# Joining two of the three matmuls of a Strassen product, and moving two weight sums to GpSimd

## The chip, the core and the metric

The kernel runs on one core of a Trainium2 chip. The core has five engines with a queue of instructions each: TensorE (PE in the profile, its weight loads are PEld), VectorE (DVE), ScalarE (ACT), GpSimd (POOL) and SyncE (SP, which here only issues DMAs). An engine takes the instructions of its queue in order; a semaphore wait of one holds back all that stand behind it. The metric is the device time of one execution in microseconds (us), the median of several runs. Lower is better.

## The reference

A streaming encoder: two layers on 512 tokens of 1024 features, all in float32. In each layer

```
x = x + 0.5 * swiglu(rms_norm(x, g1), w_gate, w_up, w_down)      # FFN 1, inner width 2816
h = rms_norm(x, gm);  p = h @ w_in
x = x + concat(attention(p), conv(p)) @ w_out                    # the mixer
x = x + 0.5 * swiglu(rms_norm(x, g2), w_gate, w_up, w_down)      # FFN 2
x = rms_norm(x, gp)

def swiglu(x, w_gate, w_up, w_down):
    return (silu(x @ w_gate) * (x @ w_up)) @ w_down
```

There are four FFNs in all. The change lies in their gate and up products; the mixer is not touched.

## The kernel before

**Split precision.** A float32 factor is held as a high part in the type that TensorE multiplies (`hi`, a cast on ScalarE) and the remainder (`lo`, a subtraction on VectorE). A product of two such factors is three matmuls that accumulate in PSUM: hi x hi, hi x lo and lo x hi (`mm3`, L152 to L154; the first two load the same weights, `wh`, and stream the activation's hi and lo part).

**An FFN.** `ffn_body` treats the inner width in four chunks of blocks, `CHUNKS = ((0, 2), (2, 5), (5, 8), (8, 11))`; a unit of a chunk is a pair of 128-wide inner blocks, gate and up. The first chunk is computed plainly, with matmuls of 512 columns. Meanwhile `operands` builds the activations' Strassen combinations for all later pairs. The other three chunks have three pairs each; each pair goes through `pair`, so that there are 9 pairs in an FFN and 36 in the kernel. After the chunks (2, 5) and (5, 8) the down projection of that chunk follows as `down`, two rounds (g = 0, 1) of seven Strassen products too, and for these chunks `pair` also builds the down operands from its results (`quartered`: the tiles b, u, v and their splits). The last chunk is followed by a plain down projection.

**A pair.** Winograd's form of Strassen: the weights come as four quarters of 128x1024 (a11, a12, a21, a22, loaded by SP), the activations as b11, b21, t2, t3, t1, t4, b22. There are seven products, in this order, each into one of three PSUM banks:

- b11 with a11 into bx, b21 with a12 into by
- t2 with s2 into bx (added to what is there), t3 with s3 into bz, t1 with s1 into bx
- t4 with a22 into bz, b22 with s4 into bx

A product is 2 (gate and up, `gu`) x 4 (k) x 3 matmuls of 128x256: gate fills columns 0 to 255 of the bank, up the columns 256 to 511. Before bx is added to again, its partial sum is copied out by ScalarE (`copied`), and VectorE combines the copies (L389, L400, L402, L406 and so on).

**The weights' side.** `split_into` makes hi (ACT, L242) and lo (DVE, L244) of a quarter or of a sum, five times in a pair. For a12 and a22, `summed` takes lo another way: ACT writes the negated hi (L366) and GpSimd issues a DMA that adds the weights from HBM to it (L367). The four sums of quarters s3, s1, s2, s4 are made in place on VectorE (L385 to L388), each 128x1024: s3 = a11 + a21, then a21 = a21 + a22, a11 = a11 + a21, a12 = a12 + a11.

**Order.** A scheduler with a time model of its own places the instructions in the queues. `tc.issue_after` adds fixed edges on one engine: products keep their order on TensorE, and the sums stand behind the last VectorE operation on the previous pair's t1 product (`order["first"]`). Pools set the rest: 7 PSUM banks, 4 weight tiles `wh` and 4 `wl`, 4 quarter tiles `fr`, 3 `raw` (a12 and s3 lie there), 2 `ls`, 5 `tmps`.

Of the kernel before, what the change touches and what calls it, by code (L numbers as in the profile page):

```python
# [7 lines left out]
FP = mybir.dt.float32  # L8
# [7 lines left out]
P = 128  # L16
# [41 lines left out]
ORDER = "t0s1p3v4o5"  # L58

# [13 lines left out]
def encoder_kernel(ctx: ExitStack, tc: tile.TileContext, xT, consts, vecs, rgain, wgu1, wd1, wdq1,  # L73
# [11 lines left out]
    def nm(s):  # L85
        uid[0] += 1
        return f"{s}{uid[0]}"
# [163 lines left out]
    def ffn_body(fpool, l, gx, norm, wgu, wd, wdq, gain, done, w0, halved):  # L251
# [52 lines left out]
        def operands(R):  # L304

            def halved(src, own=False):
                hi, lo = (fpool.tile([P, S], FR, tag="xs", name=nm("xs"), bufs=2) if own else slot(FR)
                          for _ in range(2))
                h3, l3 = (v.rearrange("p (j t) -> p j t", j=2) for v in (hi, lo))
                A.copy(h3, src)  # L310
                V.tensor_tensor(l3, src, h3.bitcast(FP), ALU.subtract)
                return hi, lo
# [5 lines left out]
            for i in range(2):  # L318
# [7 lines left out]
                for n, src in (("b11", b11), ("b21", b21)):  # L326
                    X[n].append(halved(src))
                    yield
# [4 lines left out]
                X["t2"].append(halved(t2))  # L333
                yield
                X["t3"].append(halved(t3))
# [3 lines left out]
                X["t1"].append(halved(t1))  # L339
# [3 lines left out]
                X["t4"].append(halved(t4))  # L343
                yield
                X["b22"].append(halved(b22, i == 1))
                yield

        def product(o, w, n, start, stop):
            with tc.issue_after(order["pe"]):
                for gu in range(2):  # L350
                    for k in range(4):
                        hi, lo = X[n][k // 2]
                        t = slice(k % 2 * HS, (k % 2 + 1) * HS)
                        c = slice(gu * 512 + k * P, gu * 512 + (k + 1) * P)
                        last = mm3(o[:, gu * HS:(gu + 1) * HS], w[0][:, c], w[1][:, c], hi[:, t], lo[:, t],
                                   start and gu == 0 and k == 0, stop and k == 3, True)
            order["pe"] = last

        def copied(o, src):
            A.copy(o, src)  # L360
            return o

# [14 lines left out]
        def pair(p, quartered):  # L377

            a11, a12, a21, a22, s3 = quarters(wgu[l, p], WC, p == CHUNKS[0][1])
            bx, by, bz = bank(), bank(), bank()  # L380
# [3 lines left out]
            with after("first"):  # L384
                V.tensor_tensor(s3, a11, a21, ALU.add)  # L385
                V.tensor_tensor(a21, a21, a22, ALU.add)
                V.tensor_tensor(a11, a11, a21, ALU.add)  # L387
                V.tensor_tensor(a12, a12, a11, ALU.add)  # L388
            V.tensor_tensor(a, a, by, ALU.add)  # L389
            s = tmp()  # L390
            A.activation(s[:, 0:HS], a[:, 0:HS], AF.Silu)
# [3 lines left out]
            copied(r2[:, 0], bx)  # L395
            product(bz, split_into("s3", s3), "t3", True, True)
            d = copied(tmp(), bz)
            product(bx, split_into("s1", a21), "t1", False, True)
# [808 lines left out]
```

## Time and profile before

| what | value |
|---|---|
| median of 3 runs (lowest to highest) | 1806.97 us (1805.7 to 1807.44) |
| span of the profiled execution | 1803.8 us, 3.2 us under the median |
| TensorE busy, matmuls | 1786.7 us (99%), 12198 |
| VectorE busy | 1423.3 us (79%) |
| ScalarE busy | 1088.8 us (60%) |
| GpSimd busy | 422.2 us (23%) |
| one matmul 128x256, mean duration in the record | 282 ns |
| one matmul 128x512 (L153), mean duration in the record | 389 ns |

The span runs from the first instruction's start to the last one's end in one profiled execution; the median is of whole executions. Matmuls are pipelined, so the duration in a record is longer than the time from one matmul's start to the next one's; what a matmul costs in a full queue is read from successive starts in the timeline. A row of the timeline is: start and length in us, engine, line, operation, written tile <- read tiles, shape, and in brackets the idle time ahead of it with what ended it. A row of the windows has, for each engine, the busy time in that stretch and the number of instructions.

### The profile page before, as it was taken

The page shows a single profiled execution, that of the slowest core. Times are in us where ns is not written, and L with a number is a line of the kernel's source. Part 1 is how long each engine was busy: PE and PEld are TensorE (multiplying, and loading weights), DVE is VectorE, ACT ScalarE, POOL GpSimd, SP SyncE. Part 2 cuts the span into 40 slices and gives each one's busy share as a digit, 9 for nine tenths or more (in the row PEclk, how much of TensorE's full clock was granted, in tenths as well). Part 3 has the DMA queues.
Part 4 walks back from the last instruction along what each step waited for, and adds up shares of the span by engine and source line. Part 5 has one row for each costly group of instructions (what it writes and reads, how often), then busy time and mean ns, then how long its engine had stood idle before and what let it go on. Part 6 is the DMA issues. An engine that isn't in the chain of part 4 may idle for free.

```text
span 1803.8 us, 30598 instructions
## 1 busy us (share of the span) xinstructions
PE 1786.7 (99%) x12198; PEld 1645.8 (91%) x12198; DVE 1423.3 (79%) x1975; ACT 1088.8 (60%) x1685; POOL 422.2 (23%) x343
## 2 busy tenths in 40 slices
PE   9999999999999999999999999999999999999998
PEld 7899999888788899999888999998978788999997
DVE  7888887588956979887779888866999668888873
ACT  5565656457953565656635656554779535656564
POOL 1000000258843000000310000002589410000001
PEclk9999999999999999999999999999999999999999
DMA  5657574324102466664326575743250126575742
GB/s 172 165 132 193 123 187 112 108 88 135 31 24 99 126 163 162 151 163 126 123 65 170 122 195 121 194 110 110 80 147 6 52 79 167 129 189 126 187 112 73
DMA packets 70415, 226.23 MB, mean 125 GB/s; under 512 B 7936, under 2 KB 8320, under 8 KB 70272
## 3 DMA queue, kind: packets, MB, share of 16 engines
q1 hardware_dynamic: 54000, 169.74, 28.1%
q0 software_dynamic: 16128, 54.53, 17.7%
q8 instruction: 95, 1.56, 0.4%
q14 instruction: 48, 0.39, 0.1%
q10 hardware_dynamic: 144, 0.00, 0.0%
HBM read 222.15 MB, written 2.10 MB: 124 GB/s over the span
## 4 chain that ended last, share of the span: by engine, by line
PE 80%; DVE 8%; ACT 5%; POOL 3%; issue 3%; DMA 1%; SPq 0%; ACTq 0%; POOLq 0%; DVEq 0%
PE ps L154 26%; PE ps L152 25%; PE ps L153 25%; POOL y L896 2%; PE ps L834 1%; DVE wl L244 1%; ACT pr L892 1%; DVE x L449 1%; DVE r L160 1%; ACT r L806 1%; PE ps L800 1%; DVE wl L142 1%; DVE cv L888 1%; DMA raw<-in_wgu 1%; ACT wh L136 1%
## 5 line engine op out<-in xcount | busy, mean ns | idle before, releaser
L153 PE MATMUL ps<-r,wh 128*128 128x256 f32 (+1 forms) x3436 | 1062.3, 309 | 0.1
L152 PE MATMUL ps<-r,wh 128*128 128x256 f32 (+1 forms) x3436 | 1061.0, 311 | 0.6 <-ACT r L159 0.3
L154 PE MATMUL ps<-r,wl 128*128 128x256 f32 (+1 forms) x2668 | 845.6, 318 | 2.6 <-DVE wl L142 1.2
L152 PEld LDWEIGHTS ps<-r,wh 128*128 128x128 f32 x3436 | 650.9, 190 | 38.6 <-ACT wh L136 2.1
L153 PEld LDWEIGHTS ps<-r,wh 128*128 128x128 f32 x3436 | 652.3, 190 | 36.4 <-issue 2.4
L154 PEld LDWEIGHTS ps<-r,wl 128*128 128x128 f32 x2668 | 506.9, 190 | 41.3 <-DVE wl L142 3.0
L136 ACT CAST wh<-raw 128x1024 fp32r<-128x1024 f32 (+3 forms) x148 | 132.1, 900 | 211.0 <-issue 101.3
L367 POOL DMA_DIRECT2D ls<-in_wgu x72 | 62.5, 869 | 741.7 <-ACT ls L366 615.3
L242 ACT CAST wh<-fr 128x1024 fp32r<-128x1024 f32 (+1 forms) x160 | 157.6, 985 | 101.5 <-DVE fr L387 39.7
L142 DVE TENSOR_TENSOR wl<-raw,wh 128x1024 fp32r<-128x1024 f32 (+3 forms) x132 | 146.8, 1117 | 91.0 <-ACT wh L136 90.0
L154 PE MATMUL ps<-r,ls 128*128 128x256 f32 x768 | 216.7, 282 | 0.0
L244 DVE TENSOR_TENSOR wl<-fr,wh 128x1024 fp32r<-128x1024 f32 (+1 forms) x160 | 182.9, 1143 | 40.3 <-ACT wh L242 40.3
L896 POOL TENSOR_TENSOR y<-y,pr 128x511 f32<-128x511 f32 (+14 forms) x120 | 157.4, 1312 | 54.6 <-ACT pr L892 47.4
L154 PEld LDWEIGHTS ps<-r,ls 128*128 128x128 f32 x768 | 145.2, 189 | 0.0
L244 DVE TENSOR_TENSOR wl<-raw,wh 128x1024 fp32r<-128x1024 f32 (+1 forms) x100 | 113.7, 1137 | 24.6 <-ACT wh L242 24.1
L189 POOL TENSOR_TENSOR r<-r,t 128x512 f32<-128x512 f32 x45 | 77.4, 1728 | 172.7 <-ACT t L185 171.9
L242 ACT CAST wh<-raw 128x1024 fp32r<-128x1024 f32 (+1 forms) x100 | 97.9, 979 | 27.9 <-PE ps L153 19.9
L366 ACT ACTIVATE ls<-fr 128x1024 fp32r<-128x1024 f32 (+1 forms) x56 | 56.1, 1002 | 78.6 <-PE ps L154 65.2
L892 ACT ACTIVATE pr<-r,vec 128x511 f32<-128x511 f32 (+14 forms) x120 | 85.3, 735 | 10.1 <-POOL y L896 10.1
L888 DVE SCALAR_TENSOR_TENSOR cv<-r,vec,cv 128x511 f32<-128x511 f32 (+14 forms) x120 | 88.0, 733 | 3.4 <-ACT cv L884 2.1
L449 DVE SCALAR_TENSOR_TENSOR x<-ps,x 128x512 f32<-128x512 f32 x112 | 77.1, 689 | 15.8 <-PE ps L154 15.4
L367 POOL DMA_DIRECT2D ls<-in_wdq x32 | 27.6, 863 | 260.5 <-ACT ls L366 260.5
(220 smaller groups left out, 2441.5 us busy)
## 6 DMA issues: line engine op xcount, KB each, us to landing
fr<-in_wgu SPq DMA_DIRECT2D x112, 512.0 KB, 3.4
ls<-in_wgu POOLq DMA_DIRECT2D x72, 512.0 KB, 6.3
raw<-in_wgu SPq DMA_DIRECT2D x62, 512.0 KB, 5.0
fr<-in_wdq SPq DMA_DIRECT2D x48, 384.0 KB, 4.6
ls<-in_wdq POOLq DMA_DIRECT2D x32, 384.0 KB, 4.7
raw<-in_wd SPq DMA_DIRECT2D x32, 384.0 KB, 3.1
raw<-in_wd SPq DMA_DIRECT2D x32, 256.0 KB, 2.7
raw<-in_wcv SPq DMA_DIRECT2D x16, 512.0 KB, 3.2
```

Of the source, the lines that this page charges most:

```text
L136: order["cast"] = A.copy(hi[:, :w], raw[:, :w]).ins
L142: (G if kind in POOLW.split() else V).tensor_tensor(lo[:, :w], raw[:, :w], hi[:, :w].bitcast(FP), ALU.subtract)
L152: T.matmul(o, lh, rh, start=first, stop=False, skip_group_check=free)
L153: T.matmul(o, lh, rl, start=False, stop=False, skip_group_check=free)
L154: order["mm"] = T.matmul(o, ll, rh, start=False, stop=last, skip_group_check=free).ins
L242: A.copy(hi[:, :w], src[:, :w])
L244: order["lo"] = V.tensor_tensor(lo[:, :w], src[:, :w], hi[:, :w].bitcast(FP), ALU.subtract).ins
L367: G.dma_start(out=lo[:, :n], in_=w, accum_op=ALU.add)
L449: return V.scalar_tensor_tensor(v, o.rearrange("p (m t) -> p m t", m=2), 0.5 * sign, v, ALU.mult, ALU.add).ins
L888: V.scalar_tensor_tensor(acc[:, s:], u[c][:, :S - s], tap(k), acc[:, s:], ALU.mult, ALU.add)
L892: A.activation(pr[:, s:], u[c][:, :S - s], AF.Copy, scale=tap(k))
L896: order["conv"] = G.tensor_tensor(acc[:, s:], acc[:, s:], pr[:, s:], ALU.add).ins
```

## The change

1. The activations' hi and lo halves of one 256-column block now lie side by side in one 512-wide tile (`both`), made by a cast and a subtraction of 256 columns each, where one cast and one subtraction of 512 columns served two blocks.
2. A gate/up pair uses six banks, three for gate and three for up. In six of the seven products (all but b11) hi x hi and hi x lo become one matmul of 512 columns into a whole bank, followed by lo x hi of 256 columns into its first half. The second half of a bank, the rest, holds the hi x lo sum.
3. So the results are read in parts: `copied` copies the first halves (two of 256 columns, where it was one of 512), and VectorE adds or subtracts the rests, 256 columns at a time. The result of the last product, once read by ScalarE and VectorE from the bank, is copied and completed first (`y`).
4. Two of the four weight sums, s3 = a11 + a21 and a12 = a12 + a11, go from VectorE to GpSimd.

```diff
--- before.py
+++ after.py
@@ -56,6 +56,7 @@
 WOP = 4
 EVP = "DAD"
 ORDER = "t0s1p3v4o5"
+JOINED = ("b21", "t2", "t3", "t1", "t4", "b22")
 
 VECS = [("g1", 8), ("gm", 8), ("g2", 8), ("gp", 8), ("gql", 3), ("gkl", 2),
         ("cw", 4 * CK), ("cb", 4), ("lg", 4), ("lb", 4), ("gq", 1), ("gk", 1)]
@@ -304,12 +305,13 @@
         def operands(R):
 
             def halved(src, own=False):
-                hi, lo = (fpool.tile([P, S], FR, tag="xs", name=nm("xs"), bufs=2) if own else slot(FR)
-                          for _ in range(2))
-                h3, l3 = (v.rearrange("p (j t) -> p j t", j=2) for v in (hi, lo))
-                A.copy(h3, src)
-                V.tensor_tensor(l3, src, h3.bitcast(FP), ALU.subtract)
-                return hi, lo
+                made = []
+                for j in range(2):
+                    both = fpool.tile([P, S], FR, tag="xs", name=nm("xs"), bufs=2) if own else slot(FR)
+                    A.copy(both[:, 0:HS], src[:, j])
+                    V.tensor_tensor(both[:, HS:S], src[:, j], both[:, 0:HS].bitcast(FP), ALU.subtract)
+                    made.append(both)
+                return made
 
             def diff(a, b, op=ALU.subtract):
                 t = tmp().rearrange("p (j t) -> p j t", j=2)
@@ -324,41 +326,51 @@
                         yield
                 b11, b12, b21, b22 = (v[:, :, h * HS:(h + 1) * HS] for v in (e, o) for h in range(2))
                 for n, src in (("b11", b11), ("b21", b21)):
-                    X[n].append(halved(src))
+                    X[n].extend(halved(src))
                     yield
                 t3 = diff(b12, b22)
                 yield
                 t2 = diff(t3, b11)
                 yield
-                X["t2"].append(halved(t2))
+                X["t2"].extend(halved(t2))
                 yield
-                X["t3"].append(halved(t3))
+                X["t3"].extend(halved(t3))
                 yield
                 t1 = diff(b11, b12)
                 yield
-                X["t1"].append(halved(t1))
+                X["t1"].extend(halved(t1))
                 yield
                 t4 = diff(b21, t2, ALU.add)
                 yield
-                X["t4"].append(halved(t4))
+                X["t4"].extend(halved(t4))
                 yield
-                X["b22"].append(halved(b22, i == 1))
+                X["b22"].extend(halved(b22, i == 1))
                 yield
 
-        def product(o, w, n, start, stop):
+        def product(os, w, n, start, stop):
             with tc.issue_after(order["pe"]):
-                for gu in range(2):
+                for gu, o in enumerate(os):
                     for k in range(4):
-                        hi, lo = X[n][k // 2]
-                        t = slice(k % 2 * HS, (k % 2 + 1) * HS)
+                        both = X[n][k]
                         c = slice(gu * 512 + k * P, gu * 512 + (k + 1) * P)
-                        last = mm3(o[:, gu * HS:(gu + 1) * HS], w[0][:, c], w[1][:, c], hi[:, t], lo[:, t],
-                                   start and gu == 0 and k == 0, stop and k == 3, True)
+                        first, end = start and k == 0, stop and k == 3
+                        if n in JOINED:
+                            T.matmul(o, w[0][:, c], both, start=first, stop=False, skip_group_check=True)
+                            last = T.matmul(o[:, 0:HS], w[1][:, c], both[:, 0:HS], start=False, stop=end,
+                                            skip_group_check=True).ins
+                        else:
+                            last = mm3(o[:, 0:HS], w[0][:, c], w[1][:, c], both[:, 0:HS], both[:, HS:S],
+                                       first, end, True)
             order["pe"] = last
 
-        def copied(o, src):
-            A.copy(o, src)
+        def copied(o, os):
+            for gu in range(2):
+                A.copy(o[:, gu * HS:(gu + 1) * HS], os[gu][:, 0:HS])
             return o
+
+        def parts(os):
+
+            return [(slice(gu * HS, (gu + 1) * HS), o[:, 0:HS], o[:, HS:S]) for gu, o in enumerate(os)]
 
         def subtracted(w, src, n=WC):
 
@@ -377,36 +389,51 @@
         def pair(p, quartered):
 
             a11, a12, a21, a22, s3 = quarters(wgu[l, p], WC, p == CHUNKS[0][1])
-            bx, by, bz = bank(), bank(), bank()
+            bx, by, bz = ((bank(), bank()) for _ in range(3))
             product(bx, split_into("a11", a11), "b11", True, True)
             a = copied(tmp(), bx)
             product(by, summed(wgu[l, p, 1], a12), "b21", True, True)
             with after("first"):
-                V.tensor_tensor(s3, a11, a21, ALU.add)
+                G.tensor_tensor(s3, a11, a21, ALU.add)
                 V.tensor_tensor(a21, a21, a22, ALU.add)
                 V.tensor_tensor(a11, a11, a21, ALU.add)
-                V.tensor_tensor(a12, a12, a11, ALU.add)
-            V.tensor_tensor(a, a, by, ALU.add)
+                G.tensor_tensor(a12, a12, a11, ALU.add)
             s = tmp()
-            A.activation(s[:, 0:HS], a[:, 0:HS], AF.Silu)
+            for c, main, rest in parts(by):
+                V.tensor_tensor(a[:, c], a[:, c], main, ALU.add)
+                V.tensor_tensor(a[:, c], a[:, c], rest, ALU.add)
+                if c.start == 0:
+                    A.activation(s[:, 0:HS], a[:, 0:HS], AF.Silu)
             V.tensor_tensor(s[:, 0:HS], s[:, 0:HS], a[:, HS:S], ALU.mult)
             product(bx, split_into("s2", a11), "t2", False, True)
             r2 = wide(fpool.tile([P, WC], FP, tag="e", name=nm("e"), bufs=1))
             copied(r2[:, 0], bx)
+            for c, _, rest in parts(bx):
+                V.tensor_tensor(r2[:, 0, c], r2[:, 0, c], rest, ALU.add)
             product(bz, split_into("s3", s3), "t3", True, True)
             d = copied(tmp(), bz)
+            for c, _, rest in parts(bz):
+                V.tensor_tensor(d[:, c], d[:, c], rest, ALU.add)
             product(bx, split_into("s1", a21), "t1", False, True)
             copied(r2[:, 1], bx)
-            order["first"] = V.tensor_tensor(r2[:, 1], d, r2[:, 1], ALU.subtract).ins
+            V.tensor_tensor(r2[:, 1], d, r2[:, 1], ALU.subtract)
+            for c, _, rest in parts(bx):
+                order["first"] = V.tensor_tensor(r2[:, 1, c], r2[:, 1, c], rest, ALU.subtract).ins
             product(bz, summed(wgu[l, p, 3], a22), "t4", False, True)
-            V.tensor_tensor(r2[:, 0], bz, r2[:, 0], ALU.subtract)
+            for c, main, rest in parts(bz):
+                V.tensor_tensor(r2[:, 0, c], main, r2[:, 0, c], ALU.subtract)
+                V.tensor_tensor(r2[:, 0, c], rest, r2[:, 0, c], ALU.add)
             s2 = tmp()
             s2v = s2.rearrange("p (h t) -> p h t", h=2)
             A.activation(s2v, r2[:, :, 0:HS], AF.Silu)
             V.tensor_tensor(s2v, s2v, r2[:, :, HS:S], ALU.mult)
             product(bx, split_into("s4", a12), "b22", False, True)
-            A.activation(s[:, HS:S], bx[:, 0:HS], AF.Silu)
-            V.tensor_tensor(s[:, HS:S], s[:, HS:S], bx[:, HS:S], ALU.mult)
+            y = copied(tmp(), bx)
+            for c, main, rest in parts(bx):
+                V.tensor_tensor(y[:, c], y[:, c], rest, ALU.add)
+                if c.start == 0:
+                    A.activation(s[:, HS:S], y[:, c], AF.Silu)
+            V.tensor_tensor(s[:, HS:S], s[:, HS:S], y[:, HS:S], ALU.mult)
             if not quartered:
                 return [split(s), split(s2)]
             h0, h1 = slice(0, HS), slice(HS, S)
```

## The prediction

> **What bounds the kernel now.** I read the page's busy shares and the chain first, then TensorE's groups in a stretch of Strassen work, then the engines' busy time pair by pair.
>
> ```profile
> PE 1786.7 (99%) x12198; PEld 1645.8 (91%) x12198; DVE 1423.3 (79%) x1975; ACT 1088.8 (60%) x1685; POOL 422.2 (23%) x343
> PE 80%; DVE 8%; ACT 5%; POOL 3%; issue 3%; DMA 1%; SPq 0%; ACTq 0%; POOLq 0%; DVEq 0%
> ```
>
> TensorE is the bound. Groups of TensorE between 78 and 300 us, which is nearly two quartered chunks and some of the last (name | busy us, mean ns | idle before):
>
> ```profile
> L152 PE MATMUL ps<-r,wh 128*128 128x256 f32 x587 | 165.8, 282 | 0.0
> L154 PE MATMUL ps<-r,wl 128*128 128x256 f32 x408 | 115.6, 283 | 0.2
> ```
>
> It waits 0.2 us there: every operand comes in time. How near the others are shows in stretches of one pair: three pairs of chunk (2, 5), its down, then the three pairs of the last chunk (per engine: busy us, instructions):
>
> ```profile
> 74.50:94.60 20.10, 20.10 (x170) 20.06 (x170) 14.68 (x17) 12.35 (x16) 1.73 (x2) 1.00 0.53 158
> 94.60:114.80 20.20, 20.20 (x172) 20.20 (x171) 17.18 (x25) 14.27 (x20) 1.73 (x2) 1.00 0.60 144
> 114.80:134.90 20.10, 20.10 (x171) 20.10 (x170) 17.45 (x26) 14.52 (x22) 1.72 (x2) 1.00 0.53 126
> 134.90:165.10 30.20, 30.08 (x252) 29.87 (x251) 27.65 (x38) 16.08 (x21) 3.09 (x4) 1.00 0.71 187
> 255.90:275.90 20.00, 20.00 (x169) 20.00 (x169) 13.69 (x15) 12.05 (x15) 1.94 (x3) 1.00 0.62 159
> 275.90:296.10 20.20, 20.20 (x172) 20.20 (x171) 15.00 (x19) 13.46 (x18) 1.72 (x2) 1.00 0.51 124
> 296.10:316.00 19.90, 19.90 (x164) 19.63 (x163) 13.99 (x18) 11.92 (x17) 0.00 (x0) 1.00 0.42 106
> ```
>
> A pair takes 20.1 us. VectorE (the fourth figure) is busy for 17.2 to 17.5 us of it in the second and third pair of a quartered chunk: 3 us of room, in the stages that the change touches.
>
> **TensorE's part.** What a matmul costs is the step from start to start. Two rows of the timeline, 60 matmuls of 256 columns apart, and two 21 matmuls of 512 apart:
>
> ```profile
> 303.00 0.28 PE L154 MATMUL ps<-r,wl 128*128 128x256 f32 x1
> ...
> 310.20 0.28 PE L154 MATMUL ps<-r,wl 128*128 128x256 f32 x1
> ...
> 319.04 0.39 PE L153 MATMUL ps<-r,wh 128*128 128x512 f32 x1
> ...
> 323.80 0.39 PE L153 MATMUL ps<-r,wh 128*128 128x512 f32 x1
> ```
>
> 7.20 / 60 = 120 ns and 4.76 / 21 = 227 ns. A joined matmul takes the place of two: 240 - 227 = 13 ns saved. There are 36 x 6 x 8 = 1728 of them: 22.5 us, 0.62 us a pair. So TensorE alone needs 19.5 us a pair. Bounds: nothing saved, if a 256 behind a 512 takes more than 120 ns, to the 22.5. I take 22.5, since successive 256s and successive 512s are both measured here.
>
> The Trainium skill (TensorE: Matmul & The Clock Gate, Back-to-back issue gap) gives the warm gap as columns / 2.4 ns + 2.5 ns, so that a matmul less would save only the 2.5 ns. By that the saving would be 1728 x 2.5 ns = 4.3 us, 0.12 us a pair in place of 0.62, and the sum below 8 us higher (sixteen pairs that TensorE paces, 0.5 each). The trace does not agree: with a weight load before each matmul it shows 120 and 227 ns, a fixed part of 13 ns.
>
> **VectorE's part.** Its queue in the second pair, with idle time in brackets:
>
> ```profile
> 104.40 1.22 DVE L244 TENSOR_TENSOR wl<-raw,wh 128x1024 fp32r<-128x1024 f32 x1 [0.49 <-ACT wh L242]
> ...
> 110.65 0.69 DVE L400 TENSOR_TENSOR e<-t,e 128x512 f32<-128x512 f32 x1 [1.81 <-ACT e L360]
> 111.26 1.22 DVE L385 TENSOR_TENSOR raw<-fr,fr 128x1024 f32<-128x1024 f32 x1
> 112.39 0.69 DVE L402 TENSOR_TENSOR e<-ps,e 128x512 f32<-128x512 f32 x1
> 112.99 1.22 DVE L386 TENSOR_TENSOR fr<-fr,fr 128x1024 f32<-128x1024 f32 x1
> ...
> 117.93 0.43 DVE L418 TENSOR_TENSOR u<-t,t 128x256 f32<-128x256 f32 x1
> 118.26 0.43 DVE L420 TENSOR_TENSOR t<-t 128x256 f32<-128x256 f32 x1
> 118.60 1.23 DVE L244 TENSOR_TENSOR wl<-fr,wh 128x1024 fp32r<-128x1024 f32 x1
> 119.73 1.23 DVE L244 TENSOR_TENSOR wl<-raw,wh 128x1024 fp32r<-128x1024 f32 x1
> ```
>
> From start to start: 256 columns 0.335 us, 512 0.60, 1024 1.13. In a pair the change adds sixteen operations of 256 that read PSUM (a: 4, after t2: 2, t3: 2, t1: 2, t4: 4, b22: 2) = 5.36 us, and removes two of 512 = 1.20 and two sums of 1024 = 2.26. Net +1.9 us: the second pair needs 17.18 + 1.9 = 19.1 us. In the third pair's stretch only one of the two moved sums falls (a12's; the next sums belong to down and stay), so 17.45 + 5.36 - 1.20 - 1.13 = 20.5.
>
> **The sums on GpSimd are not free for VectorE.** This decides. Before, GpSimd does no arithmetic in the FFNs; the mixer shows what a 1024-wide operation does there. From the timeline:
>
> ```profile
> 532.69 2.41 POOL L142 TENSOR_TENSOR wl<-raw,wh 128x1024 fp32r<-128x1024 f32 x1 [15.17 <-PE ps L153]
> ...
> 542.39 2.85 POOL L142 TENSOR_TENSOR wl<-raw,wh 128x1024 fp32r<-128x1024 f32 x1
> ...
> 542.90 0.68 DVE L945 TENSOR_TENSOR x<-x,ps 128x512 f32<-128x512 f32 x1
> 543.50 2.83 DVE L142 TENSOR_TENSOR wl<-raw,wh 128x1024 fp32r<-128x1024 f32 x1
> ```
>
> An operation takes GpSimd 2.41 us, 2.85 when it starts under one of VectorE's. VectorE's subtraction of two SBUF operands, 1.22 us elsewhere, takes 2.83: GpSimd ends at 545.24, it ends at 546.33, 1.09 later. It stood for the whole of GpSimd's operation. The one that reads PSUM beside it (L945) takes 0.68, as always. So a sum on GpSimd stops every VectorE operation with two SBUF operands, and all that queue behind it.
>
> In the built queues of the changed kernel, GpSimd's s3 sum for the next pair waits for the split of s4 on VectorE (its tile is a12's). Behind that split stand one PSUM read (0.34) and then a split with two SBUF operands: 2.41 - 0.34 = 2.1 us lost. GpSimd's a12 sum waits for VectorE's a11 sum. Behind that stand three PSUM reads (1.0) and then an SBUF product: 1.4 us lost. Together 3.5 us of the 4.8; the bounds are 1.75 (half of it meets waits that VectorE has anyway, as the 1.81 above) and 2 x 2.85 = 5.7. I take 3.5.
>
> **The sum.** VectorE's queue also gates TensorE: bx may be added to again only when its rests are read, so its lag comes back within a pair. In a quartered chunk:
> - first pair: 14.68 + 1.9 + 3.5 = 20.1, but its first sum meets VectorE's waits for the first products: 19.6, -0.5 on 20.1
> - second: 17.18 + 1.9 + 3.5 = 22.6, +2.4
> - third: 20.5 + 1.4 (one sum) = 21.9, +1.8
> - hand-over to down: in before, u's lo comes out at the moment its product could start:
>
> ```profile
> 138.50 0.69 DVE L160 TENSOR_TENSOR r<-u,r 128x512 fp32r<-128x512 f32 x1
> ...
> 139.23 0.28 PE L154 MATMUL ps<-r,wl 128*128 128x256 f32 x1
> ```
>
> The chain from the last product to it gains two copies and one addition, some 0.6 us (0.335 + 0.3), with no cover; to this comes whatever VectorE is behind, up to 2 us. I take 1.3.
>
> That is +5.0 a chunk, and there are 8: +40 us. Down itself keeps its 252 matmuls.
>
> In the last chunk, which makes no u and v: 13.69 + 1.9 + 3.5 = 19.1, so TensorE's 19.5; 15.00 + 5.4 = 20.4; 13.99 + 3.0 + 1.4 = 18.4, so 19.5; +0.6 at the end: 60.0 for 60.1. Nothing.
>
> The operands' splits, 14 a FFN, become two of 256: 2 x 0.335 - 0.60 = 0.07 us each, 1 us a FFN on VectorE beside plain matmuls. I cost it at nothing, covered by the matmuls; uncovered, 4 us. ScalarE's copies go from four of 512 to ten of 256. Its steps from start to start:
>
> ```profile
> 104.28 0.58 ACT L360 COPY e<-ps 128x512 f32<-128x512 f32 x1
> 104.76 0.42 ACT L391 ACTIVATE t<-t 128x256 f32<-128x256 f32 x1
> 105.07 0.61 ACT L159 CAST r<-t 128x512 fp32r<-128x512 f32 x1
> ```
>
> 10 x 0.31 - 4 x 0.48 = +1.2 us on 14.3: covered by the pair's 19.5, and what stands at the end of a chunk is in the hand-over.
>
> Sum: 1803.8 + 40 = 1844 span; with the 3.2 us between span and median, 1847 us. The saving of 22.5 us is inside these figures: 0.62 in each pair that TensorE still paces, lost in the others.
>
> **GpSimd's queue.** It also issues the DMAs that make lo for a12 and a22, now behind the s3 sum:
>
> ```profile
> 102.75 0.86 POOL L367 DMA_DIRECT2D ls<-in_wgu  x1 [8.59 <-ACT ls L366]
> ...
> 117.76 0.28 PE L154 MATMUL ps<-r,ls 128*128 128x256 f32 x1
> ...
> ls<-in_wgu POOLq DMA_DIRECT2D x72, 512.0 KB, 6.3
> ```
>
> The one at 102.75 serves the b21 product, whose first matmul on `ls` starts at 117.76, 15.0 us later. In the changed queue it stands behind the next pair's s3 sum, which can start when the split of s4 is done (the row at 104.40, so 105.6) and takes 2.41: issue at 108.0, landing 6.3 us later at 114.3. 3.5 us are left, so I cost it at nothing, covered as long as the landing takes under 9.8 us.
>
> **Rivals.**
> (a) Faster: VectorE keeps up, because GpSimd's sums fall into its idle time and what is too much in a third pair runs over into down, which has 30.2 - 27.65 = 2.5 us of room. The second pair has 19.5 - 19.1 = 0.4 us left, so this holds only if less than 0.4 of the 4.8 us is lost. For it: 1.81 us of idle in the queue shown. Against: the 2.83 us row. Then every pair takes 19.5: 8 x (-1.9 + 0.6) and 4 x (-1.6 + 0.6) = -14 us, 1793; with the hand-over covered too, 1807 - 22.5 = 1784.5. By the gap of the Trainium skill (TensorE: Matmul & The Clock Gate, Back-to-back issue gap) the last case would give 1802.7, faster still, though barely. Chance 0.13.
> (b) About even: a quarter of the lock is felt, 0.9 us a pair. First pair 19.6, second 20.0, third 20.5 + 0.35 = 20.9, hand-over 0.6: +0.7 a chunk, 8 x 0.7 - 4 x 1.0 = +2 us, 1809. It needs VectorE's idle time to lie just behind both sums. Chance 0.04 (within 0.2%, 3.6 us, about what a measurement of this kernel can tell).
> (c) Much slower: the lo DMAs come late and b21 waits. With VectorE 2 us behind at the split of s4, a sum of 2.85 and a landing 3 us longer than the median, the lo part is there at 114.3 + 2 + 0.4 + 3 = 119.7. That is 1.9 us after the need, in 24 quartered pairs 46 us on top: 1893. For it: the order of GpSimd's queue. Against: 6.3 is the middle of 72 landings, and a slower pair moves the need back. Chance 0.05.
>
> **How the numbers follow.** The likeliest, 1847, has 0.78. Its own range goes by the bounds of the lock. At 1.75 us: 19.6, 20.8, 21.2 and 0.6 for the hand-over are +1.8 a chunk, 8 x 1.8 - 4 x 1.0 = +10, 1817. At 5.7 us: 22.3, 24.8, 20.5 + 2.85 = 23.4 and 0.6 are +10.7 a chunk, 86 us, 1893. Faster by over 0.2% has 0.13 from (a), within it 0.04 from (b), slower 0.83. The range from 1806 to 1897 takes in (b) and leaves out (a) and the worse half of (c).
>
> **What would show it.** Starts 227 and 120 ns apart in joined products (TensorE's part); VectorE operations with two SBUF operands of 2 to 3.5 us beside GpSimd's sums, and PSUM reads unchanged at 0.42 (the lock); TensorE waiting on VectorE's reads of bx and bz by 2 to 3 us in second and third pairs (the sum); waits on `ls` would mean (c). No such long operations, or TensorE without waits in the pairs, would make me wrong, as would VectorE idle in the second pairs.

## The result, and the profile after

The changed kernel takes 1855.02 us, the median of 5 runs (1852.7 to 1857.02), beside 1806.97 us for the kernel before in the same session: a ratio of 1.0267, with a 95% interval from 1.0255 to 1.028. It is slower by 48 us. The execution that was profiled took 1855.32 us with a span of 1853.6 us.

The busy shares and the chain of the page after, to be read against those of before:

```profile
PE 1803.7 (97%) x10470; PEld 1560.7 (84%) x10470; DVE 1592.2 (86%) x2463; ACT 1129.5 (61%) x1957; POOL 597.2 (32%) x415
PE 59%; DVE 26%; issue 6%; ACT 6%; POOL 3%; DMA 1%; ACTq 0%; SPq 0%; DVEq 0%; POOLq 0%
```

TensorE runs 1728 matmuls fewer and is yet busy for 17 us more; its busy time alone does not show that it has lost its pace, the chain does, where its share fell from 80% to 59%. VectorE went from 1423.3 to 1592.2 us, and its share of the chain from 8% to 26%.

The engines' busy time by stretches of one pair, in the same order as before: the three pairs of chunk (2, 5), its down, then the three pairs of the last chunk.

```profile
77.70:97.90 20.20, 19.96 (x121) 17.43 (x120) 18.89 (x26) 12.95 (x21) 6.58 (x4) 1.00 0.54 157
97.90:119.50 21.60, 20.63 (x122) 17.48 (x121) 21.60 (x36) 15.29 (x26) 6.52 (x4) 1.00 0.56 135
119.50:139.80 20.30, 19.66 (x118) 16.90 (x117) 20.30 (x37) 14.47 (x26) 4.15 (x3) 1.00 0.53 124
139.80:172.60 32.80, 32.07 (x259) 31.08 (x258) 30.19 (x43) 17.34 (x23) 5.79 (x5) 1.00 0.68 173
258.00:277.80 19.80, 19.80 (x147) 18.88 (x146) 17.75 (x20) 12.14 (x17) 10.02 (x6) 1.00 0.83 235
277.80:298.80 21.00, 20.48 (x124) 17.84 (x123) 19.21 (x29) 14.75 (x25) 6.93 (x4) 1.00 0.54 125
298.80:319.00 20.20, 19.84 (x119) 17.51 (x120) 18.96 (x31) 12.89 (x23) 3.28 (x2) 1.00 0.44 92
```

In the second and third pair VectorE (the fourth figure) has no idle time left: 21.60 of 21.60 us and 20.30 of 20.30. It, not TensorE, sets their length. The view of TensorE's waits names what it waits for (us in all, times, longest):

```profile
PE ps L358 <- DVE e L412: 12.0, 29, 0.8
PE ps L155 <- DVE wl L143: 6.2, 4, 2.1
...
PE ps L358 <- DVE t L416: 3.3, 10, 0.9
PE ps L358 <- DVE e L421: 3.2, 9, 0.4
```

L358 is the joined matmul; L412, L416 and L421 are VectorE's reads of the rests, which free a bank. L143 is something else: weights of ordinary products, outside the pairs.

A ledger shows where the 49.8 us of span went. As a mark I take the first matmul on an `ls` tile in the b21 and t4 product of each pair, and in the products of down that have one. Four of them, for the second pair, the third, and the first part of down:

```profile
101.06 0.28 PE L359 MATMUL ps<-r,ls 128*128 128x256 f32 x1
...
122.68 0.28 PE L359 MATMUL ps<-r,ls 128*128 128x256 f32 x1
...
142.95 0.28 PE L155 MATMUL ps<-r,ls 128*128 128x256 f32 x1
...
153.27 0.28 PE L155 MATMUL ps<-r,ls 128*128 128x256 f32 x1
```

So the second pair takes 122.68 - 101.06 = 21.6 us, from the third pair to down it is 20.3, and the first part of down 10.3. The same differences over the whole trace, in us; the first four columns are means over the 8 quartered chunks, the last four the sums of what was gained or lost against the kernel before (the leads are what lies between the last pair of one FFN and the first pair of the next, with the beginning and the end of the program):

| kernel | pair 1 | pair 2 | pair 3 to down | down, first part | chunks | last chunks | leads | span |
|---|---|---|---|---|---|---|---|---|
| before | 20.05 | 20.05 | 19.33 | 8.99 | 0 | 0 | 0 | 0 |
| after | 20.17 | 21.67 | 20.28 | 10.32 | +32.5 | -0.2 | +17.4 | +49.8 |
| all sums on VectorE | 19.84 | 21.22 | 20.70 | 10.32 | +29.1 | -2.4 | +16.8 | +43.6 |
| two sums left out | 19.84 | 19.83 | 19.56 | 10.33 | +9.0 | -5.1 | +13.5 | +17.3 |
| before with two sums on GpSimd | 20.17 | 20.94 | 19.33 | 8.99 | +8.7 | 0.0 | +1.0 | +9.7 |
| before with operands split in halves | 20.06 | 20.05 | 19.33 | 8.99 | +0.4 | 0.0 | +2.2 | +2.6 |
| before with the joined layout | 20.05 | 20.05 | 19.33 | 8.99 | +0.1 | 0.0 | +9.0 | +9.0 |
| after, casts in turn | 21.00 | 21.64 | 20.28 | 10.32 | +39.5 | -0.4 | +5.0 | +44.1 |
| after, one sum more on GpSimd | 22.22 | 23.54 | 22.51 | 10.32 | +81.8 | +27.8 | +13.7 | +123.3 |
| joined in the last chunk only | 20.41 | 20.05 | 19.33 | 8.99 | +2.9 | -2.4 | +7.9 | +8.4 |

Two thirds of the loss lie in the quartered chunks, as forecast. One third lies in the leads, where the change does not touch a matmul.

The lock is there in plain figures. VectorE's 36 products of two SBUF operands at L429 (duration in ns, least / median / most): 24 of them stand beside GpSimd's a12 sum for the next pair and take 2117 ns or more; the other 12, in the third pair of each chunk, have no such sum beside them and take 674 to 686. Below them the same operations in the version with all sums on VectorE (first experiment), and the changed kernel's reads of PSUM at L433, 48 of whose 72 stand beside a sum of GpSimd:

```profile
L429 DVE TENSOR_TENSOR t<-t,e x36: 674/2130/2145, 99.1 to 1809.7; 128x512 f32<-128x512 f32 x36
```

```profile
L429 DVE TENSOR_TENSOR t<-t,e x36: 683/693/731, 99.1 to 1804.4; 128x512 f32<-128x512 f32 x36
```

```profile
L433 DVE TENSOR_TENSOR t<-t,ps x72: 400/409/420, 98.5 to 1814.8; 128x256 f32<-128x256 f32 x72
```

One operation takes 2130 ns where it takes 693, a loss of 1.44 us; the reads of PSUM beside a sum take 400 to 417 ns, like the others. The timeline shows both sums at work, GpSimd's first and the operation of VectorE that stood:

```profile
106.11 2.44 POOL L397 TENSOR_TENSOR raw<-fr,fr 128x1024 f32<-128x1024 f32 x1 [5.41 <-DVE u L445]
...
106.86 1.98 DVE L446 TENSOR_TENSOR u<-u,t 128x256 f32<-128x256 f32 x1
...
119.92 2.41 POOL L400 TENSOR_TENSOR raw<-raw,fr 128x1024 f32<-128x1024 f32 x1 [0.98 <-DVE fr L399]
120.10 0.73 DVE L433 TENSOR_TENSOR t<-t,ps 128x256 f32<-128x256 f32 x2
120.76 2.12 DVE L429 TENSOR_TENSOR t<-t,e 128x512 f32<-128x512 f32 x1
```

The s3 sum (L397) costs the u operation 1.98 - 0.41 = 1.57 us. VectorE's reads of PSUM beside the a12 sum (L433) go on; the first operation with two SBUF operands ends with GpSimd's. The Trainium skill (SBUF — State Buffer, SBUF: two separate sides) states this as an exclusive lock on a shared pair of ports, held for a whole instruction against VectorE operations with two SBUF inputs. The rows above agree.

### The profile page after: what moved, and what is told of

Read it like the earlier page. It is cut to its first block, busy times and chain, and to the rows that moved or that the text cites. A ratio compares the mean times of both kernels' runs of the same rounds, so it can differ in the third digit from the quotient of the medians.

```text
span 1853.6 us, 28337 instructions
## 1 busy us (share of the span) xinstructions
PE 1803.7 (97%) x10470; PEld 1560.7 (84%) x10470; DVE 1592.2 (86%) x2463; ACT 1129.5 (61%) x1957; POOL 597.2 (32%) x415
## 4 chain that ended last, share of the span: by engine, by line
PE 59%; DVE 26%; issue 6%; ACT 6%; POOL 3%; DMA 1%; ACTq 0%; SPq 0%; DVEq 0%; POOLq 0%
PE ps L155 14%; PE ps L153 14%; PE ps L154 13%; PE ps L358 9%; DVE wl L245 6%; PE ps L359 4%; POOL y L923 2%; DVE t L429 1%; DVE fr L398 1%; DVE fr L399 1%; DVE r L161 1%; PE ps L861 1%; PE ps L827 1%; DVE e L419 1%; DVE u L446 1%
## 5 line engine op out<-in xcount | busy, mean ns | idle before, releaser
L153 PE MATMUL ps<-r,wh 128*128 128x256 f32 (+1 forms) x1852 | 617.0, 338 | 5.0 <-ACT wh L137 1.7
L154 PE MATMUL ps<-r,wh 128*128 128x256 f32 (+1 forms) x1852 | 618.7, 334 | 1.3 <-DVE r L161 1.0
L358 PE MATMUL ps<-r,wh 128*128 128x512 f32 x1584 | 566.1, 398 | 19.4 <-DVE e L412 12.0
L155 PE MATMUL ps<-r,wl 128*128 128x512 f32 (+1 forms) x1660 | 561.8, 341 | 9.6 <-DVE wl L143 6.2
L153 PEld LDWEIGHTS ps<-r,wh 128*128 128x128 f32 x1852 | 351.0, 190 | 49.6 <-ACT wh L137 4.5
L358 PEld LDWEIGHTS ps<-r,wh 128*128 128x128 f32 x1584 | 296.8, 187 | 106.3 <-DVE e L412 21.2
L154 PEld LDWEIGHTS ps<-r,wh 128*128 128x128 f32 x1852 | 351.1, 190 | 39.6 <-DVE r L161 2.9
L359 PE MATMUL ps<-r,wl 128*128 128x256 f32 x1008 | 282.2, 280 | 0.0
L137 ACT CAST wh<-raw 128x1024 fp32r<-128x1024 f32 (+3 forms) x148 | 130.9, 899 | 167.6 <-PE ps L154 76.9
L143 DVE TENSOR_TENSOR wl<-raw,wh 128x1024 fp32r<-128x1024 f32 (+3 forms) x132 | 154.1, 1176 | 75.2 <-ACT wh L137 74.1
L245 DVE TENSOR_TENSOR wl<-fr,wh 128x1024 fp32r<-128x1024 f32 (+1 forms) x160 | 202.2, 1264 | 9.1 <-ACT wh L243 8.9
L359 PEld LDWEIGHTS ps<-r,wl 128*128 128x128 f32 x1008 | 190.4, 189 | 0.2
L359 PE MATMUL ps<-r,ls 128*128 128x256 f32 x576 | 160.4, 278 | 0.0
L397 POOL TENSOR_TENSOR raw<-fr,fr 128x1024 f32<-128x1024 f32 x36 | 93.4, 2594 | 123.8 <-DMA fr<-in_wgu 55.0
L190 POOL TENSOR_TENSOR r<-r,t 128x512 f32<-128x512 f32 x45 | 73.2, 1633 | 170.8 <-ACT r L183 105.1
L245 DVE TENSOR_TENSOR wl<-raw,wh 128x1024 fp32r<-128x1024 f32 (+1 forms) x100 | 113.9, 1139 | 4.3 <-ACT wh L243 3.8
```

Source lines behind the costliest of these rows:

```text
L137: order["cast"] = A.copy(hi[:, :w], raw[:, :w]).ins
L143: (G if kind in POOLW.split() else V).tensor_tensor(lo[:, :w], raw[:, :w], hi[:, :w].bitcast(FP), ALU.subtract)
L153: T.matmul(o, lh, rh, start=first, stop=False, skip_group_check=free)
L154: T.matmul(o, lh, rl, start=False, stop=False, skip_group_check=free)
L155: order["mm"] = T.matmul(o, ll, rh, start=False, stop=last, skip_group_check=free).ins
L190: (eng or (V if last else G)).tensor_tensor(self.acc, self.acc, sq, ALU.add)
```

## The experiments

My theory: VectorE has about 3 us of room a pair; the 16 operations that read the rests and the lock of GpSimd's sums use it up, and TensorE waits for banks. The rivals: the joined work alone is the cause and GpSimd is harmless, or the loss comes from the added instructions elsewhere. Eight kernels were run, in two groups of four on one chip each; the first group stands against 1806.29 us for the kernel before, the second against 1806.85.

**All four sums back on VectorE.**

```diff
-                G.tensor_tensor(s3, a11, a21, ALU.add)
+                V.tensor_tensor(s3, a11, a21, ALU.add)
...
-                G.tensor_tensor(a12, a12, a11, ALU.add)
+                V.tensor_tensor(a12, a12, a11, ALU.add)
```

> The joined products as in the changed kernel, but all four weight sums on VectorE. Theory (GpSimd's sums hold VectorE up): in the second pair two stops cost VectorE 3.0 us (0.69 to 2.12 us at one product, 0.41 to 1.98 us at one subtraction), while two sums of its own cost 2 x 1.13 = 2.26 us. So this is faster than the changed kernel by about 0.7 us in a second pair and 0.3 in a third, 8 x 1.0 = 8 us: 1843 to 1852. Rival (GpSimd's sums take nothing from VectorE, the added reads alone fill it): VectorE gets 2.26 us more in second and 1.13 in third pairs, 8 x 3.4 = 27 us slower than the changed kernel, 1882.

Measured: 1850.84 us, ratio 1.024 (1.0225 to 1.0255). The two sums cost VectorE 2 x 1.13 = 2.26 us a pair on itself, and about as much through the lock when GpSimd does them. Moving them to GpSimd bought nothing: without that move the loss is 44.6 us against its own kernel before, instead of 48.1, a small difference, since the two intervals touch at 1.0255. The time lies in the range, but not by the steps that I had named: the second pair is 0.45 us shorter than in the changed kernel, where 0.7 was forecast, and the third 0.42 longer, where 0.3 shorter was; the last chunks gain 2.2 us and one lead loses 4.8. VectorE is full here too, without any lock, in a stretch of the second pair:

```profile
96.80:118.00 21.20, 20.19 (x122) 17.51 (x121) 21.20 (x39) 15.29 (x26) 1.72 (x2) 1.00 0.64 140
```

So the lock alone is not what makes the kernel slow. VectorE has no room for the added reads and the two sums together, whether it does the sums or stands for them.

**The sums alone on GpSimd, nothing joined.**

```diff
-                V.tensor_tensor(s3, a11, a21, ALU.add)
+                G.tensor_tensor(s3, a11, a21, ALU.add)
...
-                V.tensor_tensor(a12, a12, a11, ALU.add)
+                G.tensor_tensor(a12, a12, a11, ALU.add)
```

> The kernel before, with s3 and a12's sum on GpSimd and nothing joined. Theory: VectorE loses 3.0 us a pair to the stops and is spared 2.26, so it stands at some 18 of 20.1 us in second pairs; TensorE still paces: no change, 1804 to 1811. The long operations of two SBUF operands (about 2 us) are to be seen all the same. Rival (the handing to and fro between GpSimd and VectorE delays s2 by itself, whatever the room): TensorE waits for wl of s2, 0.5 to 1 us in 36 pairs, 1825 to 1843.

Measured: 1815.02 us, ratio 1.0046 (1.0029 to 1.0062), between the two expectations. With VectorE's room still there the lock costs 0.9 us in a second pair, 0.1 on the mean in a first, and nothing in a third or in the last chunk. Most of it shows as a wait for an eviction:

```profile
PE ps L152 <- ACT e L360: 5.1, 8, 1.0
```

Why ScalarE's copy is late there was not followed further.

**The operands' splits in halves, nothing else.**

```diff
-                A.copy(h3, src)
-                V.tensor_tensor(l3, src, h3.bitcast(FP), ALU.subtract)
+                for j in range(2):
+                    A.copy(h3[:, j], src[:, j])
+                    V.tensor_tensor(l3[:, j], src[:, j], h3[:, j].bitcast(FP), ALU.subtract)
```

> The kernel before, with only the splitting of the activations' Strassen operands into casts and subtractions of 256 columns in place of 512; products, evictions and sums as before. In the changed kernel the stretches ahead of the chunks with pairs (end of the mixer or of the FFN before, plain chunk) are 3 to 5 us longer in each FFN, 15 us in all. Theory: the 14 more operations on VectorE and ScalarE in each FFN do it, so this shows 1817 to 1824. Rival 1 (the 0.07 us each that they cost on VectorE are covered, the 15 us come from another order of the queues around the first pair): 1805 to 1811.

Measured: 1809.92 us, ratio 1.0018 (1.0009 to 1.0028). The added instructions by themselves cost 2.6 us of span (3.6 by the medians), 2.2 of it in the leads, within the 4 us that I had as a bound. They do not make the leads 15 us longer; my theory for this run falls.

**Two sums left out.** Nothing runs in their place, on either engine; everything else of the change stays.

```diff
-                G.tensor_tensor(s3, a11, a21, ALU.add)
...
-                G.tensor_tensor(a12, a12, a11, ALU.add)
...
-            product(bz, split_into("s3", s3), "t3", True, True)
+            product(bz, split_into("s3", a22), "t3", True, True)
```

> The changed kernel with s3 and a12's sum left out (s3's product reads a22 in place of the sum, a12 stays as it was loaded), so that GpSimd does no arithmetic in the FFNs and VectorE is neither stopped nor given work. Theory: second pairs fall from 21.6 us to between 19.5 and 19.9, third pairs by 0.5 to 1; 8 x 2.5 = 20 us: 1830 to 1840, the rest being the longer stretches ahead of the pairs and the hand-over to down. Rival (VectorE's sixteen added reads alone pace the pairs): under 5 us faster than the changed kernel, 1850 to 1856.

Measured: 1823.11 us, ratio 1.0086 (1.0071 to 1.0101), less than even the theory expected. The first and second pairs fall to TensorE's pace, 19.83 to 19.84 us; the third stretch falls to 19.56, still 0.23 above the kernel before, with a wait of at most 0.5 us for VectorE in each of the 8 chunks, 3.9 us in all. This run has the same 2463 instructions on VectorE as the changed kernel, so the difference in busy time is the time for which VectorE stood. The line of the page, and a stretch of one pair, in which VectorE has room again:

```profile
PE 1786.2 (98%) x10470; PEld 1558.6 (86%) x10470; DVE 1496.8 (82%) x2463; ACT 1124.9 (62%) x1957; POOL 418.2 (23%) x343
...
97.00:117.00 20.00, 19.95 (x124) 17.67 (x123) 18.95 (x37) 14.96 (x27) 1.72 (x2) 1.00 0.53 126
```

1592.2 - 1496.8 = 95.4 us, over 36 pairs 2.65 us a pair. In the ledger the quartered and the last chunks together are 32.5 - 0.2 - 9.0 + 5.1 = 28 us shorter than the changed kernel's. What is left in the quartered ones, +9.0, is the hand-over to down (1.33 us in 8 chunks = 10.6) less what the pairs save. And 13.5 of the 17.4 us of the leads stay, so most of that loss has nothing to do with the sums.

**One more sum on GpSimd.**

```diff
                 G.tensor_tensor(a12, a12, a11, ALU.add)
+                G.tensor_tensor(a12, a12, a11, ALU.add)
```

> The changed kernel with one more sum on GpSimd in each pair: a11 is added to a12 a second time, right behind the first (so the product b22 reads a12 + 2 a11 where it should read a12 + a11). VectorE's and ScalarE's work is the same. Theory (a GpSimd sum holds up every operation of VectorE with two SBUF operands): in the second and third pairs, where VectorE sets the pace, 1.4 to 2.4 us more each; first pairs, which have some room, 0 to 1.5; the last chunk 1 to 3 us. That is 8 x (2.8 to 6.3) + 4 x (1 to 3) = +26 to +62 us: 1881 to 1917 us. Rival (GpSimd's sums run beside VectorE, and only VectorE's added operations of 256 columns set the second pairs): 1852 to 1860 us.

Measured: 1927.57 us, ratio 1.0662 (1.0645 to 1.068), above the range of my theory and far from the rival's. Its VectorE does the same work as the changed kernel's; the line of the page, and two rows of the timeline:

```profile
PE 1819.9 (94%) x10470; PEld 1564.8 (81%) x10470; DVE 1672.5 (87%) x2463; ACT 1127.7 (59%) x1957; POOL 700.4 (36%) x451
```

```profile
102.74 2.75 POOL L401 TENSOR_TENSOR raw<-raw,fr 128x1024 f32<-128x1024 f32 x1
103.14 3.43 DVE L245 TENSOR_TENSOR wl<-fr,wh 128x1024 fp32r<-128x1024 f32 x1
```

VectorE stands for 1672.5 - 1592.2 = 80.3 us more, 2.2 us for each added sum. A split of weights, 1.21 us elsewhere, takes 3.43 beside it. The 123.3 - 49.8 = 73.5 us of added span are 2.0 us a sum. With no room left in VectorE, a GpSimd sum costs most of its length of 2.75 us. This shows that the lock, not only the reads of the rests, sets the time. A part of the added span may have another way: the split of s4 now waits for one sum more, and TensorE waits 15.5 us for a lo of weights (PE ps L359 <- DVE wl L245), which it does not do in the changed kernel. The 80.3 us for which VectorE stands do not depend on that.

**The leads: the layout alone.** The order on ScalarE had changed. In the leads of the kernel before, ScalarE alternates casts of operands (L310) with casts of the plain chunk's weights (L136); in the changed kernel (L311, L137) the weights come last:

```profile
61.15 0.60 ACT L310 CAST r<-t 128x512 fp32r<-128x512 f32 x1
61.66 1.14 ACT L136 CAST wh<-raw 128x512 fp32r<-128x512 f32 x2
62.70 0.62 ACT L310 CAST r<-t 128x512 fp32r<-128x512 f32 x1
63.22 0.62 ACT L136 CAST wh<-raw 128x512 fp32r<-128x512 f32 x1
```

```profile
60.47 1.31 ACT L311 CAST r<-fr 128x256 fp32r<-128x256 f32 x4
61.68 2.55 ACT L311 CAST r<-t 128x256 fp32r<-128x256 f32 x8
64.14 1.66 ACT L137 CAST wh<-raw 128x512 fp32r<-128x512 f32 x3
...
64.81 0.50 PE L153 MATMUL ps<-r,wh 128*128 128x512 f32 x1 [1.14 <-ACT wh L137]
...
68.04 0.50 PE L155 MATMUL ps<-r,wl 128*128 128x512 f32 x1 [1.47 <-DVE wl L143]
```

Twelve casts of operands run ahead of the three of weights, and TensorE waits 1.14 us for the one and 1.47 for VectorE's half of the next. The test takes the kernel before and gives its operands the tiles of the changed one:

```diff
-                A.copy(h3, src)
-                V.tensor_tensor(l3, src, h3.bitcast(FP), ALU.subtract)
-                return hi, lo
+                for j in range(2):
+                    both = fpool.tile([P, S], FR, tag="xs", name=nm("xs"), bufs=2) if own else slot(FR)
+                    A.copy(both[:, 0:HS], src[:, j])
+                    V.tensor_tensor(both[:, HS:S], src[:, j], both[:, 0:HS].bitcast(FP), ALU.subtract)
+                    made.append(both)
+                return made
...
-                        hi, lo = X[n][k // 2]
-                        t = slice(k % 2 * HS, (k % 2 + 1) * HS)
+                        both = X[n][k]
...
-                        last = mm3(o[:, gu * HS:(gu + 1) * HS], w[0][:, c], w[1][:, c], hi[:, t], lo[:, t],
+                        last = mm3(o[:, gu * HS:(gu + 1) * HS], w[0][:, c], w[1][:, c], both[:, 0:HS], both[:, HS:S],
```

> The kernel before with one part of the change only: each operand's hi and lo of one half stand side by side in one 512-wide tile (the change's layout, with its 28 splits of 256 columns), but nothing is joined, the four sums stay on VectorE and a product keeps one PSUM bank. In the changed kernel the stretches between the last chunk of one FFN and the first pair of the next are some 11 to 15 us longer in all. In the built queue of ScalarE this layout alone already puts the operands' casts in blocks of four and eight ahead of the weights' casts, as in the changed kernel. Theory (this order makes the weights of the plain chunk late): these stretches grow here as in the run without the two sums, +2.5, +3.9, +2.7 and +2.2 us, so 1814 to 1821 us, with pairs unchanged at 20.05 us and waits of TensorE on the wl of the plain chunk of about 6 us. Rival (the joined products, or their six PSUM banks a pair, make those stretches long): as with the split operands alone, 1807 to 1812 us.

Measured: 1815.08 us, ratio 1.0044 (1.0029 to 1.0059). Nothing is joined here, the pairs are those of before, and the leads are 9.0 us longer. The same block of casts stands ahead of the weights:

```profile
61.49 2.55 ACT L310 CAST r<-t 128x256 fp32r<-128x256 f32 x8
63.94 1.66 ACT L136 CAST wh<-raw 128x512 fp32r<-128x512 f32 x3
```

So a change of tiles moved the order of a queue, and the two together cost 9.0 us; the splits alone, above, cost 2.6. That the rest is the order is argued from these rows and from the next run; no run changed the order alone. Why the planner chose it was not tried.

**The leads: the changed kernel with the casts in turn.**

```diff
-                    A.copy(both[:, 0:HS], src[:, j])
+                    with tc.issue_after(order["cast"]):
+                        A.copy(both[:, 0:HS], src[:, j])
```

> The changed kernel, with each operand's cast on ScalarE queued behind the last weight cast that the program issued before it. In the built queue the casts of the plain chunk's weights then stand between pairs of operand casts again, as in the kernel before, and nothing else of the change is taken back. Theory (the order of the casts makes the weights late): the stretches ahead of the first pairs give back 7 to 13 us, the pairs stay at 19.84, 21.6 and 20.3 us: 1841 to 1848 us. Rival (the joined products or their banks make them long): 1852 to 1858 us, as the changed kernel.

Measured: 1849.04 us, ratio 1.0228 (1.0211 to 1.0245), 1 us above the theory's range. The leads do what it said: +17.4 becomes +5.0, and the leads ahead of the first, second and fourth FFN are back at +0.2, +0.2 and 0.0 us. But 7 us of these 12.4 come back behind them, in the first pair of the first chunk, 22.4 us in the second and fourth FFN instead of 19.84, and 23.5 in the third instead of 22.1. TensorE now waits there instead: in the second and fourth FFN 1.0 us for a copy of ScalarE and 0.7 for the lo of that pair's weights, in the third 2.1 us for the lo:

```profile
PE ps L360 <- DVE wl L245: 3.4, 3, 2.1
...
PE ps L359 <- ACT t L369: 2.0, 2, 1.0
```

So the order of the casts moves the wait; undoing it gains 5.7 us of span, not 12.4.

**Joined only where there is room.** The last chunk joins its products, with all sums on VectorE; the quartered chunks keep three matmuls a product. The casts are in turn.

```diff
+            s, s2 = (plain_pair if quartered else joined_pair)(p)
```

> A version that joins products only where VectorE had room: in the last chunk of each FFN, with all four sums on VectorE; the pairs of the two quartered chunks are those of the kernel before (three matmuls, one bank a product). The operands keep the joined layout, and their casts wait for the weights' casts as in the version with casts in turn. Theory: quartered chunks 90.66 us as before; the last chunk's pairs 19.84 and 19.94 us and the rest 11.68 us as with all sums on VectorE, 0.6 us less an FFN; its tail +0.6; the stretches ahead of the first pairs +0 to +1.5 us each: 1805 to 1812 us. Rival (the stretches stay long because of joined products somewhere in the program): 1815 to 1821 us.

Measured: 1812.71 us, ratio 1.0031 (1.0019 to 1.0043): 0.7 us above what I expected, and slower than the kernel before. The last chunks gain 2.4 us in all. The first pairs lose 2.9, and the kernel loses 7.5 in one lead, ahead of the third FFN, where TensorE waits for a sum of squares of the norm; in the other kernels that join, this lead is longer too, by 3.3 us (the changed one) to 8.1 (all sums on VectorE). The wait, and then the busy times and the granted clock of that place (the third figure from the end):

```profile
PE ps L197 <- DVE r L190: 4.3, 1, 4.3
```

```profile
900.00:907.40 7.40, 7.40 (x34) 6.01 (x32) 3.02 (x2) 7.03 (x13) 6.53 (x6) 1.00 0.27 85
907.40:911.90 4.50, 0.27 (x2) 0.00 (x0) 3.44 (x3) 3.11 (x5) 3.96 (x3) 0.83 0.14 29
911.90:915.40 3.50, 3.44 (x16) 3.44 (x17) 2.07 (x5) 0.00 (x0) 1.04 (x1) 0.50 0.54 187
915.40:920.60 5.20, 5.20 (x13) 4.13 (x14) 1.79 (x5) 0.00 (x0) 1.01 (x1) 0.50 0.00 0
920.60:926.00 5.40, 5.40 (x25) 4.40 (x24) 0.00 (x0) 0.00 (x0) 0.00 (x0) 1.00 0.00 0
```

What makes the norm's sums late in these kernels was not settled. No version that was run beats the kernel before.

## Why the prediction came out

The forecast was 1847 us with slower at 0.83; it is 1855 and slower. The mechanism held in the quartered chunks: the added reads, and what the lock takes in place of the sums, fill VectorE, and TensorE waits for it. That the number lies so near is in part luck: the quartered chunks came 7.5 us cheaper than forecast and the leads 17.4 dearer, and these errors cancel in part. TensorE's waits on the reads of the rests are 18.5 us in all; shared among the 16 second and third pairs alone that is 1.2 each, where I had said 2 to 3.

- **TensorE's part** was mis-sized. I took 13 ns a join. In a pair that VectorE does not hold up, 168 matmuls in 20.05 us became 120 in 19.84. That is 0.21 us a pair, not 0.62. A stall of 0.28 us at the start of the b22 product takes part of it, in these rows of the changed kernel's last chunk:

```profile
283.76 0.28 PE L359 MATMUL ps<-r,ls 128*128 128x256 f32 x1
284.09 0.47 PE L358 MATMUL ps<-r,wh 128*128 128x512 f32 x1
284.39 0.28 PE L359 MATMUL ps<-r,wl 128*128 128x256 f32 x1
284.51 0.40 PE L358 MATMUL ps<-r,wh 128*128 128x512 f32 x1
```

  The steps of 0.33 and 0.30 us at 284.09 and 284.39 are about 0.12 and 0.23 elsewhere, and the trace names no releaser for them. Without that stall it is (0.21 + 0.28) / 48 = 10 ns a join: a 512 in front of a 256 takes a median of 230 ns from start to start and the 256 behind it 117, 347 together, where three of 256 take 20.05 / 168 x 3 = 358. By the gap that the Trainium skill states (TensorE: Matmul & The Clock Gate, Back-to-back issue gap) it would be 2.5 ns; the rows stand nearer to mine. The net of 0.21 us a pair lies nearer to the 0.12 that I had worked out from the page, but through the stall and not through the gap.
- **VectorE's part and the lock.** I had 3.5 us lost a pair, and 2.65 were lost on the mean over 36 pairs (1.57 + 1.44 = 3.0 in a second pair). The a12 sum cost 1.4 us, as forecast, behind the very reads of PSUM that I named. The s3 sum I had placed behind the split of s4, with 2.1 us lost. That was wrong: the sum starts at 106.11, behind a subtraction for u (the releaser that its row names is L445), and the split of s4 starts only 4 us later, in this row:

```profile
110.09 1.21 DVE L245 TENSOR_TENSOR wl<-raw,wh 128x1024 fp32r<-128x1024 f32 x1
```

  The sum meets two reads of PSUM first, and costs 1.57.
- **Second and third pair.** 21.6 us instead of 22.6. The third stretch came to 20.3 us with VectorE full, instead of 21.9. Both are VectorE's, as forecast; six of the eight first pairs, at 19.84, are TensorE's, instead of 19.6.
- **Hand-over to down.** 1.3 us forecast, 10.32 - 8.99 = 1.33 measured, and it stays at 1.33 with the two sums left out. It stays at 1.33 with all sums on VectorE as well. So it belongs to the longer chain from the last product to u, and not to VectorE's lag.
- **The chunks together**: +32.5 us instead of +40. **The last chunks** with their tails: +2 instead of 0.
- **The step that failed** is the operands' splits, costed at nothing with a bound of 4 us. I priced their instructions and held them to be covered by plain matmuls. The leads came to 17.4 us, or 15.0 without the four tails of 0.6 (0.62 at the end of the program, taken for the others too; with all sums on VectorE it is -0.05, so that the sums have a part in it). The layout accounts for 9.0, of which the number of splits makes 2.2 and the order of the casts, as argued above, the rest. The wait for the norm, with the half-speed matmuls behind it, makes up some 3 of what is left. The last 3 us have a place in the trace, though no run took them apart: half-speed matmuls behind two more waits, in the leads of the second and the fourth FFN (last section).
- **Rival (a)**, that GpSimd's sums fall into idle time, fails on L429's median of 2130 ns. It is nearly true where nothing is joined: there the lock cost 9.7 us in all. **Rival (b)**, a quarter of the lock felt, fails on 2.65 us of 4.8. **Rival (c)**, late lo DMAs, did not come about; no wait of TensorE names an `ls` tile, and the landing takes 5.6 us, where 9.8 were allowed:

```profile
ls<-in_wgu POOLq DMA_DIRECT2D x72, 512.0 KB, 5.6
```

## What to carry to other kernels

Before work is moved from VectorE to GpSimd, look at which VectorE operations will stand beside it: those with two SBUF operands stood here until the GpSimd instruction ended (2130 ns for 693), so the move frees only what falls beside reads of PSUM or into idle time. Merging matmuls pays by their fixed part, here 10 ns of 358, while each eviction that it splits costs VectorE 0.335 us for an added read; it pays only where VectorE has the room. And a change of tiles should be followed through the built queues far from the place of the change, since a planner may reorder them.

## What was not expected

After the 4.3 us wait above, the granted clock is 0.50 for the 8.7 us of two stretches, and by the mean of 0.83 for some 1.5 us at the end of the stretch before them. The sixteen 1-column matmuls take 3.4 us, and in the 5.2 us behind them only 12 matmuls of 512 columns start, where 23 would fit at 227 ns. The lead loses 7.5 us through a wait of 4.3.

The changed kernel pays for shorter waits too, in the leads of the second and the fourth FFN. The wait in the second, and the busy times and granted clock behind it:

```profile
628.44 0.50 PE L155 MATMUL ps<-r,wl 128*128 128x512 f32 x1 [2.09 <-DVE wl L143]
...
629.90:633.30 3.40, 3.40 (x9) 2.65 (x9) 1.43 (x1) 1.57 (x2) 3.15 (x2) 0.50 0.92 223
```

Behind 2.09 us of waiting the clock is 0.50 for 3.4 us, from 1.5 us after the wait on, and behind 2.13 us in the fourth FFN likewise. At half speed that is some 1.7 us lost each time, by my estimate from these rows. With the joined layout alone a wait of 2.3 us at the same place has a granted clock of 1.00 behind it, so the length of the wait does not decide by itself.

The Trainium skill (TensorE: Matmul & The Clock Gate, Part 1: The HAM clock gate) has the clock halved after an idle window of about 3.4 us. The traces agree that a wait brings it, but show it behind 2.09 us and, in the long wait, about 2.7 us after its start. The Trainium skill also gives, in the same place, about 3.4 us as the time to come back; the short waits show 3.4 us at half clock, and the long one 5.2 us of full matmuls with 3.4 us of 1-column ones ahead of them.
